# A decoder trunk with seven products for ten of eleven pairs of down projection weights, their sums made by VectorE, and another order of the token tiles

## The chip, the core and the metric

The kernel runs on one core of a Trainium2 chip. The core has TensorE (PE: matrix products, which leave their sums in eight PSUM banks of 128 x 512 floats), VectorE (DVE), ScalarE (ACT), GpSimd (POOL), and SyncE (SP), which here only issues transfers. Each engine works off its own instructions in order, and waits on the others by semaphores. The metric is the time of one execution in microseconds, lower is better.

## What is computed

A trunk of two layers over 512 tokens of 1024 floats: layer 0 mixes tokens by pooling, layer 1 by attention on keys and values that are projected from the stream after layer 0. The change lies in the feed-forward part, which each layer ends with.

```python
D_MODEL = 1024; SEQ = 512; DEPTH = 2; D_FF = 2816; CONV_WIDTH = 3

def conv_ffn(h, w_up, conv_w, conv_b, w_down):
    u = h @ w_up                              # 512x1024 @ 1024x5632
    u = causal_dwconv(u, conv_w, conv_b)      # depthwise over tokens, width 3
    a, g = jnp.split(u, 2, axis=-1)
    return (jax.nn.silu(g) * a) @ w_down      # 512x2816 @ 2816x1024

for i in range(DEPTH):
    if i == 0:
        x = x + multiscale_pool(rmsnorm(x, norm_g[i, 0]), pool_w[i], pool_scale[i])
    else:
        kv = rmsnorm(x, kv_norm) @ w_kv
        x = x + diff_attention(rmsnorm(x, norm_g[i, 0]), wq[0], lam[0], subln_g[0], wo[0], k, v, ...)
    x = x + conv_ffn(rmsnorm(x, norm_g[i, 1]), w_up[i], conv_w[i], conv_b[i], w_down[i])
return rmsnorm(x, final_norm)
```

All inputs are float32.

## The kernel before

**Products in three passes.** Every operand of a large product is split into a rounded half `hi` (ScalarE, L152) and a remainder `lo` (VectorE, L153). `mm3` then issues three matmuls: hi x hi, hi x lo, lo x hi (L171 to L173).

**Weights come in chunks** of 512 KB (`chunk`, L160): SP loads `raw` (three buffers), ScalarE makes `hi`, VectorE `lo` (rings of five buffers each). A chunk's split has to wait until TensorE has used up the chunk five places before it in the ring. Some chunks of the down projection are loaded to a "wide" tile (`wide`, L99, four buffers of 128 x 1024, tag h) in place of `raw`; the squares and scaled token tiles of the norms and the last outputs use the same four tiles.

**Up projections.** The 2816 rows of `w_down` are 22 blocks of 128, named f. For each f two chunks of `w_up` give two banks `pu` of 24 matmuls each: the gate's half and the value's half. `gate` (L387) runs the convolution on ScalarE and VectorE, then silu and the product. The first two f (`EARLY`) are made in halves of the tokens, since the second half of the tokens is normed (`sq_n`), turned by TensorE (`pt_n`) and split (`n1h`, `n1l`) while products on the first half run. `n1` is the normed input of the first FFN, `n3` that of the second, `n2` that of the attention.

**Down projection by pairs.** Two neighbouring blocks f are a pair (11 pairs, NP). A pair in plain form costs 4 token tiles x 2 halves of the output columns x 2 blocks x 3 passes. For the first `SEVEN` pairs the product is made by Strassen's scheme over two halves of the tokens (tiles 0, 1 and tiles 2, 3), two blocks of rows and two halves of columns: seven products i = 1 to 7, each on 256 tokens x 128 x 512. The left factors are "forms", sums and differences of activations: `forms_one` (L408) makes those of products 5, 6 and 3, `forms_two` (L418) those of 1, 2, 4 and 7. Forms of the first `MADE` pairs are made in the up projections (tiles `fa`, `fb`); the others are "late" and made in the down projection (tiles `hall`, and `fb`). The right factors are blocks of `w_down` or sums and differences of two blocks. Two pairs are a group g, whose weights for one product are one chunk.

**Sums of weight blocks.** `sum_weights` (L440) is called behind each gate; for products 6, 3, 7 and 4 GpSimd copies one block by a transfer to DRAM and adds the other by a second transfer (L447, `sum`), 32 transfers a layer, paced by a small POOL operation. Product 1's difference is made by VectorE in the down projection (`difference`, L484).

**Order in the down projection** (L526 to L582). First half: products 5, 6, 3 of each group, with their banks `p5`, `c2`, `p3`, then the plain pairs for column half 1. Second half: products 1, 4, 7, 2 of each group, then the plain pairs for column half 0. `put` (L510) adds a bank to the residual stream x on VectorE (L512), and `put_all` puts both banks of a product at the two places it belongs to (`PLACES`). At the end the token tiles are finished one by one, 0, 1, 2, 3: the plain pairs of a tile, its put, and `after`. In layer 0 that is `to_n2` (L586): square and norm of the tile (`vectors`), and the turning of the tile two before (`tensors`); then the value projection (`pv`, L631) begins on tiles 0 and 1, and the tiles 2 and 3 are turned between its products (L775 to L779). In layer 1 it is `finish` (L862): norm, scale and store of the output.

**What sets the order.** TensorE's order is that of the code (`manual_schedule`, L85). The start of the kernel is written by hand for all engines (`ORDER`, L30). Everything else on ScalarE, VectorE, POOL and SP is placed by the Tile scheduler, so that the diff alone doesn't tell those orders.

## Time and profile before

| what | value |
|---|---|
| time, median of 3 runs (lowest to highest) | 983.58 us (983.29 to 983.75) |
| the profiled execution: its time | 985.66 us |
| the profiled execution: its span | 983.9 us |
| granted TensorE clock, mean | 0.995 |
| TensorE matmul busy | 971.1 us, 99%, 4774 instructions |
| VectorE busy | 667.5 us, 68%, 1040 instructions |
| ScalarE busy | 464.3 us, 47%, 727 instructions |
| GpSimd busy | 152.9 us, 16%, 209 instructions |

The span is from the first to the last instruction that the profiler recorded in one execution; that execution's time holds some 1.8 us around it, and was 2.1 us above the median of the timed runs. Matmuls overlap, so a single matmul's duration is longer than the spacing of their starts, and a busy share of TensorE can be near full whatever its pace. Registers, branches and issued transfers aren't counted as busy.

### The profile page before, as it was taken

What the parts mean: (1) busy time and instruction counts of PE and PEld (TensorE: products, weight loads), DVE (VectorE), ACT (ScalarE), POOL (GpSimd) and SP (SyncE); (2) the same over time, 40 slices, a digit from 0 to 9 for tenths busy, and PEclk for the clock granted to TensorE, in tenths of its full rate; (3) what the DMA queues carried; (4) which work ended last, traced back from release to release, by engine and by line L of the source; (5) the groups of instructions that cost most, each with busy time, mean ns of one, the idle gap of its engine ahead of it and who ended that gap; (6) DMA issues with size and microseconds to landing.
All of it is one profiled execution on the core that took longest, in us unless ns stands there. A gap on an engine that the chain in (4) does not pass through costs nothing.

```text
span 983.9 us, 12623 instructions
## 1 busy us (share of the span) xinstructions
PE 971.1 (99%) x4774; PEld 822.2 (84%) x4774; DVE 667.5 (68%) x1040; ACT 464.3 (47%) x727; POOL 152.9 (16%) x209
## 2 busy tenths in 40 slices
PE   8999999999999999999999999999999999999997
PEld 8998888888888888778888887998888888888885
DVE  5777655556589756467766797686745555689764
ACT  5555433334456334346756763464433334464431
POOL 4601212121000001361220101102121212000001
PEclk8999999999999999999999999999999999999999
DMA  7335788987435532343213111336889887435422
GB/s 265 112 107 152 187 218 241 222 197 195 130 110 177 180 106 91 90 122 105 65 43 108 65 43 44 86 108 166 211 211 244 208 203 191 112 126 191 150 86 85
DMA packets 144454, 141.49 MB, mean 144 GB/s; under 512 B 4737, under 2 KB 112906, under 8 KB 144394
## 3 DMA queue, kind: packets, MB, share of 16 engines
q1 hardware_dynamic: 131082, 107.14, 34.8%
q0 software_dynamic: 13312, 33.56, 15.6%
q8 instruction: 37, 0.61, 0.2%
q14 instruction: 23, 0.19, 0.1%
HBM read 138.58 MB, written 35.65 MB: 177 GB/s over the span
## 4 chain that ended last, share of the span: by engine, by line
PE 94%; DVE 2%; DMA 1%; POOL 1%; ACT 1%; issue 1%; SPq 0%; DVEq 0%; POOLq 0%; ACTq 0%
PE pu L171 16%; PE pu L173 16%; PE pu L172 16%; PE pd L173 7%; PE pd L172 7%; PE pd L171 7%; PE sc L689 2%; PE po L718 2%; PE pw L173 2%; PE pj_k L171 1%; PE pj_k L172 1%; PE pj_k L173 1%; PE pw L172 1%; PE pw L171 1%; PE pj_q L171 1%; PE pj_q L172 1%
## 5 line engine op out<-in xcount | busy, mean ns | idle before, releaser
L153 DVE TENSOR_TENSOR lo_u<-raw_u,hi_u 128x1024 fp32r<-128x1024 f32 x84 | 103.2, 1231 | 144.2 <-ACT hi_u L152 144.0
L152 ACT CAST hi_u<-raw_u 128x1024 fp32r<-128x1024 f32 x84 | 88.3, 1053 | 147.0 <-PE pu L172 142.2
L171 PE MATMUL pu<-n3h,hi_u 128*128 128x512 f32 (+1 forms) x384 | 142.9, 372 | 0.0
L171 PE MATMUL pu<-n1h,hi_u 128*128 128x512 f32 (+1 forms) x384 | 142.8, 372 | 0.0
L172 PE MATMUL pu<-n1l,hi_u 128*128 128x512 f32 (+1 forms) x384 | 142.6, 371 | 0.0
L172 PE MATMUL pu<-n3l,hi_u 128*128 128x512 f32 (+1 forms) x384 | 142.6, 371 | 0.0
L173 PE MATMUL pu<-n1h,lo_u 128*128 128x512 f32 (+1 forms) x384 | 142.6, 371 | 0.0
L173 PE MATMUL pu<-n3h,lo_u 128*128 128x512 f32 (+1 forms) x384 | 142.6, 371 | 0.0
L173 PEld LDWEIGHTS pu<-n1h,lo_u 128*128 128x128 f32 x384 | 72.3, 188 | 12.6
L172 PEld LDWEIGHTS pu<-n3l,hi_u 128*128 128x128 f32 x384 | 72.4, 188 | 12.6
L172 PEld LDWEIGHTS pu<-n1l,hi_u 128*128 128x128 f32 x384 | 72.4, 188 | 12.5
L171 PEld LDWEIGHTS pu<-n3h,hi_u 128*128 128x128 f32 x384 | 72.3, 188 | 12.5
L173 PEld LDWEIGHTS pu<-n3h,lo_u 128*128 128x128 f32 x384 | 72.3, 188 | 12.4
L171 PEld LDWEIGHTS pu<-n1h,hi_u 128*128 128x128 f32 x384 | 72.3, 188 | 12.3
L447 POOL DMA_DIRECT2D sum<-in_w_down_dram x64 | 58.5, 913 | 150.6 <-DMA sum<-in_w_down_dram 141.9
L153 DVE TENSOR_TENSOR lo_d<-raw_d,hi_d 128x1024 fp32r<-128x1024 f32 x44 | 53.6, 1222 | 27.3 <-ACT hi_d L152 27.2
L152 ACT CAST hi_d<-raw_d 128x1024 fp32r<-128x1024 f32 x44 | 46.4, 1054 | 52.0 <-PE pd L173 36.3
L390 ACT ACTIVATE cv<-cv 128x512 f32<-128x512 f32 x44 | 27.8, 633 | 76.6 <-DVE cv L384 76.5
L171 PE MATMUL pd<-hi_d,hall 128*128 128x512 f32 x140 | 54.5, 389 | 0.0
L172 PE MATMUL pd<-lo_d,hall 128*128 128x512 f32 x140 | 54.5, 389 | 0.0
L382 ACT ACTIVATE cv<-pu,c_cb,c_cw 128x512 f32<-128x512 f32 x68 | 52.6, 774 | 0.3
L384 DVE SCALAR_TENSOR_TENSOR cv<-pu,c_cw,cv 128x510 f32<-128x510 f32 x68 | 50.9, 748 | 2.1
(197 smaller groups left out, 2035.5 us busy)
## 6 DMA issues: line engine op xcount, KB each, us to landing
raw_u<-in_w_up_dram SPq DMA_DIRECT2D x88, 512.0 KB, 4.7
sum<-in_w_down_dram POOLq DMA_DIRECT2D x64, 512.0 KB, 6.1
raw_d<-in_w_down_dram SPq DMA_DIRECT2D x28, 512.0 KB, 3.3
rs_d<-sum SPq DMA_DIRECT2D x16, 512.0 KB, 4.5
raw_d<-sum SPq DMA_DIRECT2D x16, 512.0 KB, 3.7
rs_d<-in_w_down_dram SPq DMA_DIRECT2D x8, 512.0 KB, 3.2
raw_v<-in_w_kv_dram SPq DMA_DIRECT2D x8, 512.0 KB, 3.5
raw_q<-in_wq_dram SPq DMA_DIRECT2D x8, 512.0 KB, 3.8
```

Of the source, the lines that this page charges most:

```text
L152: nc.scalar.copy(hi, src)
L153: nc.vector.tensor_tensor(lo, src, hi, ALU.subtract)
L171: nc.tensor.matmul(ps, lh, rh, start=first, stop=False)
L172: nc.tensor.matmul(ps, lh, rl, start=False, stop=False)
L173: nc.tensor.matmul(ps, ll, rh, start=False, stop=last)
L382: nc.scalar.activation(y, ps, AF.Identity, bias=w[3], scale=w[2])
L384: nc.vector.scalar_tensor_tensor(y[:, 2:], ps[:, :S - 2], w[0], y[:, 2:], ALU.mult, ALU.add)
L390: nc.scalar.activation(y, y, AF.Silu)
L447: nc.gpsimd.dma_start(out=v3(summed[g, i], 2), in_=block(g, *blk), accum_op=op)
L689: nc.tensor.matmul(ps[:, :m], qs[h, c][:, q], k[:, :m], start=not last, stop=bool(last))
L718: nc.tensor.matmul(po[h][:, qi * P:(qi + 1) * P], aT[:, kt * P:(kt + 1) * P], vt[kt][h // 4][:, (h % 4) * VD:(h % 4 + 1) * VD], start=kt = ...
```

## The change

Ten pairs in place of eight go by seven products, and the forms of four in place of three are made in the up projections. The sums of weights, with product 1's difference, are made by VectorE in ten steps during the up projections (behind the gates of f = 2, 4, ..., 20): a step takes one pair's two blocks of rows into two wide tiles (`wr`, SP), makes their sum (`wb`, L458), two sums across the columns (`wa`, L460) and a difference (into `wr`, L461) on VectorE, and POOL stores the five sums to DRAM by three transfers. A step's loads are placed on SP behind the last chunk's (`issue_after`), and the chunk loads of the down projection behind the last one of the up projections (`anchor`). In the down projection's second half the products go group by group for the first groups, then product by product for the last three (`BEHIND`), with product 7's last two groups token tile by token tile. The token tiles are finished in the order 2, 3, 0, 1 (`LAST`), and the value projection takes them in that order.

```diff
-SEVEN, MADE = 8, 3
+SEVEN, MADE = 10, 4
-SUMS = {6: ((0, 0), (0, 1)), 3: ((0, 1), (1, 1)), 7: ((1, 0), (1, 1)), 4: ((1, 0), (0, 0))}
+SUMS = 4, 3, 6, 7, 1
+LAST, BEHIND = (2, 3, 0, 1), 3
+STEPS = 2, 4, 6, 8, 10, 12, 14, 16, 18, 20
...
+    loads, anchor = [], []
     def chunk(src, a, b, name, raw=None):
...
-        nc.sync.dma_start(out=v3(raw, a), in_=src)
+        with ExitStack() as behind:
+            if anchor:
+                behind.enter_context(tc.issue_after(anchor[-1].ins))
+            loads.append(nc.sync.dma_start(out=v3(raw, a), in_=src))
...
-        def sum_weights(f, a):
-            if f < EARLY or not owing:
+        summed = [dram.tile([2 * P, len(SUMS) * S], F32, tag=f"sum{g}", bufs=2, name=f"sum{l}_{g}")
+                  for g in range(SEVEN // 2)]
+        def sum_weights(f):
+            if f not in STEPS:
                 return
-            g, i = owing.pop(0)
-            pace = nc.gpsimd.tensor_scalar(small([P, 1], f"pace{l}_{f}"), a[:, :1], 1.0, None, ALU.add)
-            with tc.issue_after(pace.ins):
-                for blk, op in zip(SUMS[i], (ALU.bypass, ALU.add)):
-                    nc.gpsimd.dma_start(out=v3(summed[g, i], 2), in_=block(g, *blk), accum_op=op)
+            kk = STEPS.index(f)
+            name = f"{l}_{kk}"
+            rows = [wide(f"wr{name}_{j}") for j in range(2)]
+            one, two = rows
+            both, across2 = wide(f"wb{name}"), wide(f"wa{name}")
+            first, last = slice(0, S), slice(S, D)
+            with tc.issue_after(loads[-1].ins):
+                for j in range(2):
+                    nc.sync.dma_start(out=rows[j], in_=w_down[l, (2 * kk + j) * P:(2 * kk + j + 1) * P, :])
+            nc.vector.tensor_tensor(both, one, two, ALU.add)
+            for r, c in (one, first), (two, last):
+                nc.vector.tensor_tensor(across2[:, c], r[:, first], r[:, last], ALU.add)
+            nc.vector.tensor_tensor(one[:, first], one[:, first], two[:, last], ALU.subtract)
+            to = summed[kk // 2][kk % 2 * P:(kk % 2 + 1) * P, :]
+            nc.gpsimd.dma_start(out=to[:, :D], in_=both)
+            nc.gpsimd.dma_start(out=to[:, D:2 * D], in_=across2)
+            nc.gpsimd.dma_start(out=to[:, 2 * D:], in_=one[:, first])
...
+        anchor.append(loads[-1])
...
-        room = {kk: [halls.pop() for _ in range(3)] for kk in range(MADE, SEVEN)}
+        room = {}
         def late_one(kk):
             if kk >= MADE:
+                room[kk] = [halls.pop() if halls else big(f"fa{l}_{kk}_{i}") for i in range(3)]
                 forms_one(kk, room[kk])
...
-        def difference(g, one, name):
-            raw, hi, lo = chunk(block(g, 1, 1), 2, S, name, wide(f"rs_{name}"))
-            nc.vector.tensor_tensor(raw, one, raw, ALU.subtract)
-            split(raw, hi, lo)
-            return hi, lo
-        def seven(i, g, w, pss, first=True, last=True):
-            for t in range(2):
+        def seven(i, g, w, pss, first=True, last=True, ts=(0, 1)):
+            for t in ts:
...
-        w0 = pair_weights(SEVEN, 1)
-        for t in (2, 3):
-            pair(c2[t - 2], t, SEVEN, w0, True)
         for g in range(SEVEN // 2):
             late_one(2 * g)
             late_one(2 * g + 1)
             seven(5, g, plain(block(g, 1, 1), f"d{l}_{g}_5")[1], p5)
-            seven(6, g, of_sum(g, 6), c2, False, False)
+            seven(6, g, of_sum(g, 6), c2, True, False)
             seven(3, g, of_sum(g, 3, True), p3)
         put_all(5, p5)
         put_all(3, p3)
         c1 = banks("12")
-        for t in (0, 1):
-            pair(c1[t], t, SEVEN, w0, True)
-        for kk in range(SEVEN + 1, NP):
+        for kk in range(SEVEN, NP):
             w = pair_weights(kk, 1)
-            late_two(MADE + kk - SEVEN - 1)
             for t in range(NT):
-                pair((c1 + c2)[t], t, kk, w, last=kk == NP - 1)
+                pair((c1 + c2)[t], t, kk, w, t < 2 and kk == SEVEN, kk == NP - 1)
...
-        for g in range(SEVEN // 2):
+        into = {1: p1, 4: p4, 2: p2, 7: c1}
+        def further(i, g):
+            w = plain(block(g, 0, 0), f"d{l}_{g}_2")[1] if i == 2 else of_sum(g, i, i == 4)
+            seven(i, g, w, into[i], True, i != 7)
+        for kk in range(MADE, MADE + NP - SEVEN):
+            late_two(kk)
+        groups = range(SEVEN // 2)
+        for g in groups:
             for kk in (2 * g, 2 * g + 1):
-                if kk >= MADE + NP - SEVEN - 1:
+                if kk >= MADE + NP - SEVEN:
                     late_two(kk)
-            raw, w2 = plain(block(g, 0, 0), f"d{l}_{g}_2")
-            w1 = difference(g, raw, f"d{l}_{g}_1")
-            end = g == SEVEN // 2 - 1
-            if end:
-                seven(2, g, w2, p2)
-            seven(1, g, w1, p1)
-            seven(4, g, of_sum(g, 4), p4)
-            seven(7, g, of_sum(g, 7, True), c1, True, False)
-            if not end:
-                seven(2, g, w2, p2)
-        put_all(2, p2)
-        put_all(1, p1, (0,))
-        put_all(4, p4, (0,))
+            if g < len(groups) - BEHIND:
+                for i in into:
+                    further(i, g)
+        for i in into:
+            for g in groups[-BEHIND:]:
+                if i != 7 or g not in groups[-2:]:
+                    further(i, g)
+            if i != 7:
+                put_all(i, into[i])
+        for t in (2, 3):
+            after(t, 1, False)
         kept = [(kk, pair_weights(kk, 0)) for kk in range(SEVEN, NP)]
+        w7 = [(g, of_sum(g, 7)) for g in groups[-2:]]
         c2 = banks("21")
-        for t in range(NT):
+        for t in LAST:
+            if t < 2:
+                for g, w in w7:
+                    seven(7, g, w, c1, True, False, (t,))
             for kk, w in kept:
                 pair((c1 + c2)[t], t, kk, w, t > 1 and kk == SEVEN, kk == NP - 1)
             put((c1 + c2)[t], t, 0)
             after(t, 0, True)
-            if t == 0:
-                put_all(1, p1, (1,))
-                put_all(4, p4, (1,))
-                for i in (2, 3):
-                    after(i, 1, False)
...
-    for t in range(NT):
+    for i, t in enumerate(LAST):
         run(value(0, t, ws))
-        if t < 2:
-            n2.tensors(t + 2)
+        if i < 2:
+            n2.tensors(LAST[i + 2])
```

VectorE's order at the start of the first FFN, before: the splits of the turned token tiles 2 and 3 (`n1l`), then that of the next weight chunk, then the first gate's convolution (`cv`).

```order
L598 TENSOR_SCALAR c_gkv<-c_gkv 128x1
L153 TENSOR_TENSOR n1l<-pt_n_620,n1h 128x4x128
L153 TENSOR_TENSOR n1l<-pt_n_625,n1h 128x4x128
L153 TENSOR_TENSOR n1l<-pt_n_630,n1h 128x4x128
L153 TENSOR_TENSOR n1l<-pt_n_635,n1h 128x4x128
L153 TENSOR_TENSOR lo_u_2_862<-raw_u_2_860,hi_u_2_861 128x1024
L383 SCALAR_TENSOR_TENSOR cv_22_788<-pu_0_560,c_cw_544,cv_22_788 128x511
```

The same place after the change:

```order
L613 TENSOR_SCALAR c_gkv<-c_gkv 128x1
L458 TENSOR_TENSOR wb_0_892<-wr_0_0_890,wr_0_1_891 128x1024
L156 TENSOR_TENSOR n1l<-pt_n_620,n1h 128x4x128
L156 TENSOR_TENSOR n1l<-pt_n_625,n1h 128x4x128
L156 TENSOR_TENSOR n1l<-pt_n_630,n1h 128x4x128
L156 TENSOR_TENSOR n1l<-pt_n_635,n1h 128x4x128
L460 TENSOR_TENSOR wa_0_893<-wr_0_0_890 128x512
L460 TENSOR_TENSOR wa_0_893<-wr_0_1_891 128x512
L461 TENSOR_TENSOR wr_0_0_890<-wr_0_0_890,wr_0_1_891 128x512
L156 TENSOR_TENSOR lo_u_2_851<-raw_u_2_849,hi_u_2_850 128x1024
```

The first step's `wb` now stands ahead of the four splits that TensorE's products on the second half of the tokens read, and the rest of the step behind them; the two loads of `wr` stand on SP's queue ahead of further chunk loads.

SP's order at the end of the up projections of layer 0, before: the last chunks of `w_up`, then those of the down projection (`sum` is the DRAM tile of sums).

```order
L166 DMA raw_u_42_2247<-in_w_up_dram 128x8x128
L166 DMA raw_u_20_2278<-in_w_up_dram 128x8x128
L166 DMA raw_u_43_2323<-in_w_up_dram 128x8x128
L166 DMA raw_u_21_2354<-in_w_up_dram 128x8x128
L166 DMA raw_d_1_8_2407<-in_w_down_dram 128x2x512
L166 DMA raw_d_0_5_2425<-in_w_down_dram 128x2x512
L166 DMA raw_d_0_6_2443<-sum_0_6_676 128x1024
L166 DMA raw_d_1_5_2486<-in_w_down_dram 128x2x512
```

The same place after the change:

```order
L174 DMA raw_u_42_2294<-in_w_up_dram 128x8x128
L174 DMA raw_u_20_2325<-in_w_up_dram 128x8x128
L457 DMA wr_9_0_2370<-in_w_down_dram 128x1024
L457 DMA wr_9_1_2371<-in_w_down_dram 128x1024
L174 DMA raw_u_43_2383<-in_w_up_dram 128x8x128
L174 DMA raw_u_21_2414<-in_w_up_dram 128x8x128
L174 DMA rs_d_0_3_2503<-sum_0_676 128x2x512
L174 DMA rs_d_1_3_2557<-sum_1_677 128x2x512
L174 DMA rs_d_2_3_2625<-sum_2_678 128x2x512
L174 DMA raw_d_0_5_2467<-in_w_down_dram 128x2x512
L174 DMA rs_d_3_3_2693<-sum_3_679 128x2x512
L174 DMA raw_d_0_6_2485<-sum_0_676 128x2x512
```

The last step's two loads stand among the last loads of `w_up`, and behind these come four chunks of product 3 (into wide tiles), ahead of or between the first chunks of products 5 and 6.

VectorE's order from the end of the down projection of layer 0 into the value projection, before: x_81 to x_84 are the token tiles 0 to 3, `x<-x,pd` is a put, `sq_n<-x` a scaling, `n2l` the split of a turned tile, `lo_v` and `lo_q` splits of weights.

```order
L209 TENSOR_SCALAR sq_n_3149<-x_81,r_n_3152 128x512 x2
L512 TENSOR_TENSOR x_82<-x_82,pd_71_2783 128x512
L209 TENSOR_SCALAR sq_n_3180<-x_82,r_n_3183 128x512 x2
L512 TENSOR_TENSOR x_83<-x_83,pd_210_3128 128x512
L153 TENSOR_TENSOR n2l<-pt_n_3215,n2h 128x4x128
L209 TENSOR_SCALAR sq_n_3207<-x_83,r_n_3210 128x512 x2
L153 TENSOR_TENSOR n2l<-pt_n_3220,n2h 128x4x128
L158 SCALAR_TENSOR_TENSOR lo_v_2_3311<-raw_v_2_3309,c_gkv,hi_v_2_3310 128x512 x2
L512 TENSOR_TENSOR x_84<-x_84,pd_211_3129 128x512
L158 SCALAR_TENSOR_TENSOR lo_v_3_3319<-raw_v_3_3317,c_gkv,hi_v_3_3318 128x512 x2
L153 TENSOR_TENSOR lo_q_3459<-raw_q_3457,hi_q_3458 128x1024
L209 TENSOR_SCALAR sq_n_3248<-x_84,r_n_3251 128x512 x2
```

The same place after the change:

```order
L217 TENSOR_SCALAR sq_n_3244<-x_83,r_n_3247 128x512 x2
L217 TENSOR_SCALAR sq_n_3259<-x_84,r_n_3262 128x512 x2
L526 TENSOR_TENSOR x_81<-x_81,pd_70_2829 128x512
L217 TENSOR_SCALAR sq_n_3286<-x_81,r_n_3289 128x512 x2
L156 TENSOR_TENSOR n2l<-pt_n_3294,n2h 128x4x128
L156 TENSOR_TENSOR n2l<-pt_n_3299,n2h 128x4x128
L161 SCALAR_TENSOR_TENSOR lo_v_2_3390<-raw_v_2_3388,c_gkv,hi_v_2_3389 128x512
L526 TENSOR_TENSOR x_82<-x_82,pd_71_2830 128x512
L161 SCALAR_TENSOR_TENSOR lo_v_2_3390<-raw_v_2_3388,c_gkv,hi_v_2_3389 128x512
L161 SCALAR_TENSOR_TENSOR lo_v_3_3398<-raw_v_3_3396,c_gkv,hi_v_3_3397 128x512 x2
L217 TENSOR_SCALAR sq_n_3327<-x_82,r_n_3330 128x512 x2
L156 TENSOR_TENSOR n2l<-pt_n_3335,n2h 128x4x128
```

The tiles 2 and 3 (x_83, x_84) are scaled first, tile 0 (x_81) next, and `n2l` of tile 2 stands behind tile 0's scaling; `lo_q` and its chunk come later.

## Rows read from the trace of the kernel before

**Rows 1.** The page, its parts 1 and 2: busy time of each engine, with the share of the span and the instructions, and the clock granted to TensorE in 40 slices, in tenths of full speed.

```profile
PE 971.1 (99%) x4774; PEld 822.2 (84%) x4774; DVE 667.5 (68%) x1040; ACT 464.3 (47%) x727; POOL 152.9 (16%) x209
...
PEclk8999999999999999999999999999999999999999
```

**Rows 2.** The waits of TensorE over the whole span, longest first: engine, line, who ended the wait; us in total, times, longest.

```profile
PE sc L689 <- DVE kl L672: 1.6, 1, 1.6
PE dps L319 <- DVE h L209: 1.4, 1, 1.4
PE warm L139 <- DVE ones L134: 1.0, 1, 1.0
PE pw L171 <- ACT oh L157: 0.8, 1, 0.8
PE pv L173 <- DVE n2l L153: 0.7, 1, 0.7
```

**Rows 3.** TensorE's timeline in the down projection of layer 0: start us, us, engine, line, operation, out<-in. The first and the last of 56 rows that follow each other without an idle time.

```profile
324.65 0.39 PE L171 MATMUL pd<-hi_d,ah 128*128 128x512 f32 x1
...
337.12 0.39 PE L172 MATMUL pd<-lo_d,fb 128*128 128x512 f32 x1
```

**Rows 4.** Busy time by stretch: the stretch, its us, then busy us (instructions) of PE, PEld, DVE, ACT and POOL, the granted clock, the DMA share and GB/s. All in layer 0: in the up projections, the fullest stretch of a pair whose forms are made there; the pair three stretches on, whose forms are made later; the rest of the up projections; then the first half of the down projection.

```profile
63.30:85.00 21.70, 21.70 (x97) 17.98 (x96) 16.98 (x25) 10.58 (x16) 2.12 (x3) 1.00 0.48 141
128.60:150.30 21.70, 21.70 (x97) 18.00 (x96) 11.92 (x14) 8.12 (x11) 5.12 (x7) 1.00 0.79 204
150.30:280.90 130.60, 130.60 (x577) 108.12 (x577) 75.71 (x92) 52.24 (x67) 18.29 (x27) 1.00 0.72 189
280.90:318.50 37.60, 37.60 (x167) 31.16 (x166) 37.27 (x58) 23.74 (x33) 0.00 (x0) 1.00 0.46 157
```

**Rows 5.** Groups of instructions between 278 and 400 us, different shapes kept apart: line, engine, operation, out<-in, count | busy us, mean ns of one | idle time before them. The last row is from the page's part 5, of the whole span.

```profile
L153 DVE TENSOR_TENSOR lo_d<-raw_d,hi_d 128x1024 fp32r<-128x1024 f32 x19 | 23.1, 1221 | 7.8 <-ACT hi_d L152 7.8
L512 DVE TENSOR_TENSOR x<-x,pd 128x512 f32<-128x512 f32 x28 | 17.9, 681 | 0.8 <-PE pd L173 0.6
L153 DVE TENSOR_TENSOR hall<-f,hall 128x512 fp32r<-128x512 f32 x5 | 3.4, 682 | 0.0
L412 DVE TENSOR_TENSOR f<-ar 128x256 f32<-128x256 f32 x5 | 2.1, 418 | 0.0
...
L384 DVE SCALAR_TENSOR_TENSOR cv<-pu,c_cw,cv 128x510 f32<-128x510 f32 x68 | 50.9, 748 | 2.1
```

**Rows 6.** The page's parts 5 and 6 on the splits of the up weights and on the loads, with the median us from issue to landing; and what the trace has of line 447, POOL's transfers (ns: shortest, median, longest).

```profile
L153 DVE TENSOR_TENSOR lo_u<-raw_u,hi_u 128x1024 fp32r<-128x1024 f32 x84 | 103.2, 1231 | 144.2 <-ACT hi_u L152 144.0
L152 ACT CAST hi_u<-raw_u 128x1024 fp32r<-128x1024 f32 x84 | 88.3, 1053 | 147.0 <-PE pu L172 142.2
...
raw_u<-in_w_up_dram SPq DMA_DIRECT2D x88, 512.0 KB, 4.7
sum<-in_w_down_dram POOLq DMA_DIRECT2D x64, 512.0 KB, 6.1
...
L447 POOL DMA_DIRECT2D sum<-in_w_down_dram x64: 738/966/1091, 78.6 to 834.6; - x64
```

**Rows 7.** Timeline of ScalarE and VectorE late in the up projections of layer 0: one chunk's split on both engines, and the next one's on VectorE.

```profile
247.79 1.05 ACT L152 CAST hi_u<-raw_u 128x1024 fp32r<-128x1024 f32 x1 [0.96 <-PE pu L172]
...
248.88 1.23 DVE L153 TENSOR_TENSOR lo_u<-raw_u,hi_u 128x1024 fp32r<-128x1024 f32 x1 [2.77 <-ACT hi_u L152]
254.31 1.22 DVE L153 TENSOR_TENSOR lo_u<-raw_u,hi_u 128x1024 fp32r<-128x1024 f32 x1 [0.66 <-ACT hi_u L152]
```

**Rows 8.** Timeline at the start of the first FFN: SP's issues, VectorE's split of the transposed token tiles 2 and 3, and on TensorE their transposes and the first product that reads them (the products between go on with tiles 0 and 1).

```profile
41.90 0.39 SPq L166 DMA_DIRECT2D raw_u<-in_w_up_dram  x1
...
47.94 2.48 DVE L153 TENSOR_TENSOR n1l<-pt_n,n1h 128x512 fp32r<-128x512 f32 x4 [2.31 <-ACT n1h L152]
...
46.69 1.91 PE L236 MATMUL pt_n<-ident,sq_n 128*128 128x128 f32 x16
...
51.31 0.28 PE L171 MATMUL pu<-n1h,hi_u 128*128 128x256 f32 x1
```

**Rows 9.** Timeline from the end of the down projection of layer 0 into the value projection: SP's load of raw_q; POOL; VectorE's scaling of token tiles 1 and 3 and the n2l behind the latter; TensorE's wait.

```profile
376.92 0.37 SPq L166 DMA_DIRECT2D raw_q<-in_wq_dram  x1
...
382.35 1.90 POOL L641 TENSOR_TENSOR raw_q<-raw_q,c_gn 128x1024 f32<-128x1024 f32 x1 [2.25 <-DMA raw_q<-in_wq_dram]
384.64 0.57 POOL L194 TENSOR_TENSOR r_n<-r_n,halfneg 128x1 f32<-128x1 f32 x1
395.64 2.13 POOL L641 TENSOR_TENSOR raw_k<-raw_k,c_gkv 128x1024 f32<-128x1024 f32 x1
...
385.24 0.88 DVE L209 TENSOR_SCALAR sq_n<-x,r_n 128x512 f32<-128x512 f32 x2 [3.26 <-POOL r_n L194]
395.52 2.52 DVE L209 TENSOR_SCALAR sq_n<-x,r_n 128x512 f32<-128x512 f32 x2 [0.77 <-POOL r_n L194]
397.97 2.47 DVE L153 TENSOR_TENSOR n2l<-pt_n,n2h 128x512 fp32r<-128x512 f32 x4
...
398.70 0.50 PE L173 MATMUL pv<-hi_v,n2l 128*128 128x512 f32 x1 [0.69 <-DVE n2l L153]
```

**Rows 10.** Timeline of the last microseconds: the last matmul, and the last step on VectorE of the chain behind it.

```profile
976.27 0.39 PE L173 MATMUL pd<-hi_d,al 128*128 128x512 f32 x1
...
979.22 1.42 DVE L875 SCALAR_TENSOR_TENSOR y<-x,fr,fg 128x512 f32<-128x512 f32 x2 [1.83 <-POOL fr L871]
```

More of the change, by code (lines that the diff above doesn't have):

```diff
@@ L401, in gate @@
                 act[f] = ah, al
-            sum_weights(f, a)
+            sum_weights(f)
         left, right = slice(0, HALF), slice(HALF, S)
@@ L432, in block @@
             return src.rearrange("(k j p) c -> j p k c", j=2, p=P)[j]
-        summed = {(g, i): dram.tile([P, 2 * S], F32, tag=f"sum{g}_{i}", bufs=2, name=f"sum{l}_{g}_{i}")
-                  for i in SUMS for g in range(SEVEN // 2)}
-        owing = list(summed)
-        def sum_weights(f, a):
-            if f < EARLY or not owing:
-                return
-            g, i = owing.pop(0)
-            pace = nc.gpsimd.tensor_scalar(small([P, 1], f"pace{l}_{f}"), a[:, :1], 1.0, None, ALU.add)
-            with tc.issue_after(pace.ins):
-                for blk, op in zip(SUMS[i], (ALU.bypass, ALU.add)):
-                    nc.gpsimd.dma_start(out=v3(summed[g, i], 2), in_=block(g, *blk), accum_op=op)
+        summed = [dram.tile([2 * P, len(SUMS) * S], F32, tag=f"sum{g}", bufs=2, name=f"sum{l}_{g}")
+                  for g in range(SEVEN // 2)]
+        def sum_weights(f):
+            if f not in STEPS:
+                return
+            kk = STEPS.index(f)
[15 more added lines that the diff above has]
+            nc.gpsimd.dma_start(out=to[:, 2 * D:], in_=one[:, first])
         for n, w in enumerate(ws):
@@ L481, in of_sum @@
         def of_sum(g, i, other=False):
-            return plain(v3(summed[g, i], 2), f"d{l}_{g}_{i}", other)[1]
-        def difference(g, one, name):
-            raw, hi, lo = chunk(block(g, 1, 1), 2, S, name, wide(f"rs_{name}"))
-            nc.vector.tensor_tensor(raw, one, raw, ALU.subtract)
-            split(raw, hi, lo)
-            return hi, lo
-        def seven(i, g, w, pss, first=True, last=True):
-            for t in range(2):
+            at = SUMS.index(i) * S
+            return plain(summed[g].rearrange("(k p) c -> p k c", p=P)[:, :, at:at + S], f"d{l}_{g}_{i}", other)[1]
+        def seven(i, g, w, pss, first=True, last=True, ts=(0, 1)):
+            for t in ts:
                 for k in range(2):
@@ L577, in ffn @@
             after(t, 0, True)
-            if t == 0:
-                put_all(1, p1, (1,))
-                put_all(4, p4, (1,))
-                for i in (2, 3):
-                    after(i, 1, False)
+        anchor.clear()
     n2 = Normed("n2", None)
@@ L589, in to_n2 @@
         n2.vectors(t)
-        if t > 1:
-            n2.tensors(t - 2)
+        if t in LAST[2:]:
+            n2.tensors(LAST[LAST.index(t) - 2])
     ffn(0, n1, cw0, [w[1:] for w in up0], pup, to_n2)
```

## The prediction, made before the changed kernel ran

> **What bounds the kernel now.** I read the busy shares first, then what TensorE waited for, then single rows. TensorE's matmul row is busy 99% of the span, at a granted clock of full speed in all slices but the first [rows 1]. A busy share alone proves little, as matmuls overlap, so the second look is at the waits: the five of the whole span add to 5.5 us, and the two that lie behind the first FFN are 1.6 and 0.7 us [rows 2]; none lies inside an up or a down projection. The third look is at the spacing of starts. In the down projection 56 matmuls of 512 columns stand in a row without a gap, from 324.65 to 337.12 us: 12.47 / 55 = 0.2267 us each [rows 3]. So a matmul taken out there is worth 0.2267 us as long as its neighbours' operands are ready, and what has to be asked of this change is whether they stay ready.
>
> **Matmuls removed.** A pair of weight rows costs 48 matmuls of 512 columns in plain form (4 token tiles, 2 dim halves, 2 row blocks, 3 passes) and 42 in seven products (7 products, 2 tiles, 2 blocks, 3 passes). Two more pairs go over to seven products, in two layers: 2 x 2 x 6 = 24 matmuls, and TensorE's program is 24 rows shorter. 24 x 0.2267 = **5.44 us**. This is sure; the rest of the working is what may be lost of it.
>
> **VectorE in the up projections.** A step (one pair's sums) is one 128x1024 and three 128x512 two-input operations. By the nearest rows, lo_d at 1221 ns and x at 681 ns [rows 5], that is 1.22 + 3 x 0.68 = 3.3 us, ten times a layer, where an inner step lies 21.8 us from the next. VectorE was busy at most 17.0 us of 21.7 while a pair's forms are made, 11.9 of 21.7 in the fourth pair, and 75.7 of 130.6 afterwards [rows 4]. The fourth pair now makes its forms there too: 0.42 x 3 + 0.68 for one half and 0.42 + 3 x 0.68 for the other [rows 5], 4.4 us. So the fullest stretches are 17.0 + 3.3 = 20.3 and 11.9 + 4.4 + 3.3 = 19.6 of 21.7 us: below full, though not by much. A delay there is covered besides: the split of a weight chunk waits for ScalarE, ScalarE waits for TensorE [rows 6], and the rows show the rhythm: hi_u begins 0.96 us after its wait began, when a chunk has been used up, 1.05 and 1.23 us later the chunk is ready [rows 7], and the ring has five places, so it is used four chunks of 24 x 0.2267 = 5.44 us later. That is some 21.8 - 2.3 = 19.5 us of lead. I take 0 for these operations; uncovered they would cost 65 us (20 x 3.3).
>
> **The queues.** A step also issues two 512 KB loads on SP and three stores on POOL. Before, POOL issued 32 copying or adding transfers a layer at 966 ns each [rows 6]; now 30 plain ones. The four wide tiles that a step uses are all there are, so the next step's loads, in SP's queue ahead of raw_u loads, wait until the stores have landed. The chain of one step, from the rows: loads 4.7 us, VectorE 3.3 plus what stands ahead of it there (up to some 5), three issues 2.9, landing 6.1 [rows 5, 6]: about 22 us at the worst, 17 at best, against 21.8 between steps. At the worst it just keeps step, and being late first eats the lead. 0 again.
>
> **Start of the first FFN.** Here the cover is thin. VectorE's new order has wb_0 ahead of the four n1l. The loads that wb_0 needs are issued where a raw_u was, at 41.9 and some 0.5 us later, and its tile comes free with the first eight of 16 transposes, at about 46.69 + 0.95 = 47.6 [rows 8]. With the landing of the same size, 4.7 us [rows 6], the data are there at 47.1; so wb_0 runs 47.6 to 48.8, the third n1l (spacing 2.48 / 4 = 0.6) is done at 50.7, and TensorE wants it from 51.43, one matmul after 51.31 [rows 8]. Nothing is lost. Bounds: no loss, and, with a landing of 9.4 us (twice the row), data at 51.8 and a loss of 51.8 + 1.2 + 1.9 - 51.4 = 3.5 us. I take 0, the nearest row.
>
> **Down projection.** First half now: 15 products of 12 matmuls, 40.8 us, with 15 splits (18.3 us), six late forms of 1.94 us (11.6), and the end of the last gates (4 operations of 0.75, two of 0.68 [rows 5]): 34.3 us of VectorE. Before, VectorE was busy 37.3 of 37.6 us there and TensorE had no gap [rows 4]. The plain pair that held one place of the ring through this half is gone, so the lead grows by one product, 2.7 us. Between the halves only one plain pair (5.4 us) is left where 60 matmuls (13.6 us) stood; the first product after it needs the banks of product 5, which ended two products earlier, and its four puts take 2.7 us; the next needs those of product 3, which has 5.4 + 2.7 us for as many puts. Second half: the eight 1.22 us differences of both layers go, the late forms are started in the first half by the new order, and chunk loads stay one per product. I take 0; the bound is one late product's puts, 2.7 us a layer.
>
> **Token order 2, 3, 0, 1 at the end of layer 0.** Before, TensorE lost 0.69 us in the value projection: n2l of token tile 1 stood in VectorE's queue behind the scaling of tile 3, which waited for POOL, and whose second half took over 2 us beside POOL's raw_k [rows 9]. In the new order tiles 2 and 3 cost TensorE 1.4 us each, and the two long ones (4.1 us) follow, so that the scaling of 2 and 3 is hidden under tile 0. The raw_q load can issue some 9 us before tile 1 ends; with its 5.4 us (376.92 to 382.35) and POOL's 1.9 and 0.9 us [rows 9] tile 0's scaling ends close to where TensorE reaches the value projection, and n2l of tile 2 is behind it, ready at about the moment it is read. raw_k's load is issued later than before, after lo_v_2, and should not meet the scaling of tile 1. So the old 0.69 goes, and 0 to 1.7 comes (1.7: the collision again, 2.1 - 0.5). I take a gain of 0.3.
>
> **Tail.** After the last matmul the chain put, square, rstd, scale, store is the same [rows 10], for tile 1 in place of 3: 0.
>
> **Sum.** 5.44 + 0.3 = 5.7 us of the profiled execution's 985.66 us (span 983.9): 979.9. The median of the timed runs is 983.58, lower by 2.1, and it is that which is forecast: 983.58 - 5.7 = **977.9 us**.
>
> [...] In [rows 9] a scaling of 128x512 that otherwise takes under 0.5 us took over 2 us while POOL read SBUF: the two engines do hold each other up. [...]
>
> **Rivals.**
> *Part is given back* at the thin places: start and value projection. For it: both leads are below 1 us. 983.58 - 5.44 + 1 to 3.5 = 979.1 to 981.6.
> *Nothing measurable is left:* puts of the first half late in both layers, 2 x 2.7 = 5.4 us, so 983.6. Against it: banks of product 5 come free early.
> *Slower, the wide tiles.* If a step's chain takes longer than the 21.8 us between steps, SP stands still before raw_u loads and each step adds to the delay. Nine steps eat the 19.5 us lead when the chain is over 21.8 + 19.5 / 9 = 24 us. At 25.5 us: 9 x 3.7 - 19.5 = 13.8 us a layer, 983.58 - 5.44 + 27.6 = 1005.7 us. For it: the sums' landing of 6.1 us and the hold-up in [rows 9]. Against it: behind the fourth pair VectorE keeps some 27% of idle time with the step in it (75.7 + 6 x 3.3 of 130.6 us [rows 4]), and POOL has nothing else to do there.
>
> **Chances.** Forecast (976.6 to 979.1) 0.66; part given back 0.18; nothing left 0.08; slower 0.08. For eight times in ten the first two are enough: 976.6 (all of 5.44, 0.69 and 0.8 for what may shrink elsewhere) to 981.6. Within 0.2% (2 us) is about what a measurement of this kernel can't tell from no change; 981.6 is its edge, so the first two count as faster, 0.84, then 0.08 same and 0.08 slower.
>
> **What would show it.** The waits should hold no wait of pd or pu over 1 us; the spacing in the down projection should still be 0.227 us, with 12 matmuls fewer a layer; VectorE busier by 30 to 40 us a layer; the pv wait gone or small; POOL's transfers still near 0.9 us. Wrong would be: a wait of pu on lo_u or on a raw_u load in the up projections (wide tiles), a wait of pu on n1l near 51 us (start), a wait of pd on a put or a split after the first half.

## The result, and the profile after

The changed kernel takes 979.0 us (median of 5 runs, 977.73 to 979.26), the kernel before 983.75 us (983.29 to 984.38): a ratio of 0.995, 95% interval 0.9935 to 0.9964, so 4.75 us less. Two further measurements on other chips gave ratios of 0.9942 and 0.9946 (experiments `a_again`, `a_third`).

The page of the changed kernel, parts 1 and 2, as in [rows 1]:

```profile
PE 965.3 (99%) x4750; PEld 817.0 (84%) x4750; DVE 725.8 (74%) x1142; ACT 473.9 (48%) x741; POOL 120.4 (12%) x173
...
PEclk9999999999999999999999999999999999999999
```

The waits of TensorE over the whole span, as in [rows 2]:

```profile
PE pp L180 <- DVE pwl L156: 1.1, 2, 0.9
PE warm L142 <- DVE ones L137: 1.0, 1, 1.0
PE dps L327 <- DVE h L217: 0.8, 1, 0.8
PE pw L179 <- ACT oh L160: 0.8, 1, 0.8
PE pp L179 <- ACT pwh L155: 0.5, 1, 0.5
PE pu L180 <- DVE n1l L156: 0.3, 1, 0.3
```

TensorE's matmul is busy 5.8 us less, VectorE 58.3 us more, POOL 32.5 us less. The waits of pv and sc of [rows 2] are gone. Behind the first up product one wait is new, and it is one that the prediction priced at nothing: pu for n1l, 0.3 us. Those on pp, dps and warm lie ahead of the first up product, where every engine's order is the same in both kernels; the one on pw is there in both.

The spacing in the down projection, two rows of TensorE's timeline in layer 0, the first and the last of 56 without idle time between, as in [rows 3]:

```profile
323.43 0.39 PE L180 MATMUL pd<-lo_d,ah 128*128 128x512 f32 x1
...
335.90 0.39 PE L181 MATMUL pd<-hi_d,fb 128*128 128x512 f32 x1
```

12.47 us / 55 = 0.2267 us, as before. To see where the 4.75 us came from, the starts of each stage's first and last matmul are read from TensorE's timeline in several profiles: of the kernel before (a second profile of it is `b_again`), of the changed one (two more are `a_again` and `a_third`), and of the version with later steps (`e3_later`). The rows run from a stage's first matmul to its last, by their starts (those of the value projection and of the scores to the first of the next stage); what lies between the rows is the same in all. All in us:

| stretch | before | b_again | after | a_again | a_third | e3_later |
|---|---|---|---|---|---|---|
| to the first up product | 37.33 | 37.58 | 38.03 | 36.85 | 36.85 | 37.01 |
| up projections, layer 0 | 242.90 | 242.89 | 243.47 | 244.50 | 245.23 | 242.89 |
| down projection, layer 0 | 109.48 | 109.48 | 106.76 | 106.76 | 106.76 | 106.76 |
| value projection | 24.65 | 24.69 | 23.69 | 23.69 | 23.69 | 23.69 |
| first scores to layer 1's FFN | 184.66 | 183.08 | 183.06 | 183.05 | 183.06 | 183.06 |
| up projections, layer 1 | 242.73 | 242.73 | 242.73 | 242.73 | 242.73 | 242.73 |
| down projection, layer 1 | 108.57 | 108.57 | 105.85 | 105.85 | 105.85 | 105.85 |
| last matmul to the span's end | 7.63 | 7.62 | 7.76 | 7.72 | 7.78 | 7.76 |

Four rows differ by kernel. The two down projections are shorter by 2.72 us each, to the hundredth in every profile. The value projection is 0.96 us shorter. The up projections of layer 0 are longer by 0.57, 1.61 and 2.34 us, 1.5 on the mean. The tail is 0.1 us longer. That makes -5.44 - 0.96 + 1.5 + 0.1 = -4.8 us, the measured difference. Of these six profiles only the first one of before has the 1.6 us among the scores, and the start differs by a microsecond between profiles of one kernel (38.03 and 36.85), so it is left out of the sum.

### The profile page after: what moved, and what is told of

Its sections match the earlier page's. It is cut to its first block, busy times and chain, and to the rows that moved or that the text cites. A ratio compares the mean times of both kernels' runs of the same rounds, so it can differ in the third digit from the quotient of the medians.

```text
span 977.3 us, 12805 instructions
## 1 busy us (share of the span) xinstructions
PE 965.3 (99%) x4750; PEld 817.0 (84%) x4750; DVE 725.8 (74%) x1142; ACT 473.9 (48%) x741; POOL 120.4 (12%) x173
## 5 line engine op out<-in xcount | busy, mean ns | idle before, releaser
L156 DVE TENSOR_TENSOR lo_d<-raw_d,hi_d 128x1024 fp32r<-128x1024 f32 x54 | 65.9, 1224 | 35.0 <-ACT hi_d L155 35.0
L155 ACT CAST hi_d<-raw_d 128x1024 fp32r<-128x1024 f32 x54 | 57.1, 1057 | 63.2 <-PE pd L181 43.3
L179 PE MATMUL pd<-hi_d,hall 128*128 128x512 f32 x156 | 60.8, 390 | 0.0
L180 PE MATMUL pd<-lo_d,hall 128*128 128x512 f32 x156 | 60.7, 389 | 0.0
L458 DVE TENSOR_TENSOR wb<-wr,wr 128x1024 f32<-128x1024 f32 x20 | 24.5, 1224 | 36.8 <-DMA wr<-in_w_down_dram 36.8
L390 ACT ACTIVATE cv<-pu,c_cb,c_cw 128x512 f32<-128x512 f32 x64 | 49.5, 773 | 0.5 <-PE pu L181 0.5
L392 DVE SCALAR_TENSOR_TENSOR cv<-pu,c_cw,cv 128x510 f32<-128x510 f32 x64 | 47.9, 748 | 1.5
```

The source lines that it names most:

```text
L155: nc.scalar.copy(hi, src)
L156: nc.vector.tensor_tensor(lo, src, hi, ALU.subtract)
L179: nc.tensor.matmul(ps, lh, rh, start=first, stop=False)
L180: nc.tensor.matmul(ps, lh, rl, start=False, stop=False)
L390: nc.scalar.activation(y, ps, AF.Identity, bias=w[3], scale=w[2])
L392: nc.vector.scalar_tensor_tensor(y[:, 2:], ps[:, :S - 2], w[0], y[:, 2:], ALU.mult, ALU.add)
```

## Where the new wait comes from

SP's timeline of the changed kernel at the start of the first FFN (start us, us, operation, count), then VectorE's, ScalarE's `n1h`, then TensorE's first product that reads the third n1l; they answer to [rows 8]:

```profile
42.62 0.83 SPq L457 DMA_DIRECT2D wr<-in_w_down_dram  x2
43.55 0.38 SPq L174 DMA_DIRECT2D raw_u<-in_w_up_dram  x1
...
49.52 1.23 DVE L458 TENSOR_TENSOR wb<-wr,wr 128x1024 f32<-128x1024 f32 x1 [3.19 <-DMA wr<-in_w_down_dram]
50.67 2.48 DVE L156 TENSOR_TENSOR n1l<-pt_n,n1h 128x512 fp32r<-128x512 f32 x4
...
48.02 2.06 ACT L155 CAST n1h<-pt_n 128x512 fp32r<-128x512 f32 x4 [5.31 <-PE pt_n L244]
...
52.60 0.39 PE L180 MATMUL pu<-n1l,hi_u 128*128 128x256 f32 x1 [0.32 <-DVE n1l L156]
```

And busy time by stretch at this place: PE, PEld, DVE, ACT, POOL, granted clock, DMA share, GB/s:

```profile
42.00:46.00 4.00, 4.00 (x36) 4.00 (x35) 3.29 (x10) 0.71 (x2) 2.57 (x4) 1.00 0.86 266
46.00:48.00 2.00, 2.00 (x19) 2.00 (x19) 0.33 (x2) 0.00 (x0) 0.00 (x0) 1.00 0.96 335
48.00:50.00 2.00, 2.00 (x20) 2.00 (x19) 0.47 (x1) 1.98 (x4) 0.00 (x0) 1.00 0.74 227
```

The two loads of `wr` are issued at 42.62 us and right behind, and `wb` begins at 49.52, 6.9 us behind the first one's issue, where 5.7 us were forecast (41.9 to 47.6). Three loads of 512 KB now stand where one stood, and the transfer engines are 96% and 74% busy in the stretches 46 to 48 and 48 to 50 us; in the kernel before they were at 7% and nothing. That the loads are slow because they stand together is read from these shares; no run took one of the three away. VectorE stands still for 3.19 us ahead of `wb`, with the four n1l behind it, whose operands come ready from ScalarE's `n1h`, begun at 48.02. In `a_third` the same rows read:

```profile
42.41 0.83 SPq L457 DMA_DIRECT2D wr<-in_w_down_dram  x2
...
50.11 1.23 DVE L458 TENSOR_TENSOR wb<-wr,wr 128x1024 f32<-128x1024 f32 x1 [4.80 <-DMA wr<-in_w_down_dram]
...
53.19 0.39 PE L180 MATMUL pu<-n1l,hi_u 128*128 128x256 f32 x1 [2.08 <-DVE n1l L156]
```

There `wb` begins 7.7 us after the first load's issue, and TensorE, which was earlier by 1.2 us at its first up product, waits 2.1 us. So an early start isn't kept: it ends in this wait.

## The experiments

**The matmuls: eight pairs as before, with three pairs' forms made early and eight steps of sums; everything else changed.**

```diff
-SEVEN, MADE = 10, 4
+SEVEN, MADE = 8, 3
-STEPS = 2, 4, 6, 8, 10, 12, 14, 16, 18, 20
+STEPS = 2, 4, 6, 8, 10, 12, 14, 16
```

> The changed kernel with eight pairs by seven products and three with forms made early, as before; everything else of the change stays (VectorE's sums in eight steps, the new product order, the new token order). Theory A (the gain is the 24 matmuls at 0.2267 us, the rest of the change nearly cancels: 1.0 us gained at the value projection, 0.6 us lost at the start): 5.4 us above the changed kernel's 979.0, so 984.4 us, each down projection 2.72 us longer than the changed kernel's 106.8 and 105.9 us. Theory B (the gain comes from the other edits, the order of products and tiles): within 1 us of 979.0.

Measured: 987.1 us (986.79 to 988.98). The two down projections take 109.48 and 108.57 us, 2 x 2.72 above the changed kernel, as theory A has it. It is off by 2.7 us elsewhere, of which 1.9 us lie in the value projection, where this mixture of old and new has a wait of its own. Two of TensorE's waits:

```profile
PE pv L180 <- DVE lo_v L161: 1.3, 1, 1.3
...
PE pu L180 <- DVE n1l L156: 0.9, 1, 0.9
```

and VectorE and POOL ahead of that wait:

```profile
395.76 3.05 DVE L161 SCALAR_TENSOR_TENSOR lo_v<-raw_v,c_gkv,hi_v 128x512 fp32r<-128x512 f32 x2
...
395.95 2.30 POOL L656 TENSOR_TENSOR raw_q<-raw_q,c_gn 128x1024 f32<-128x1024 f32 x1 [1.03 <-DVE sq_n L217]
```

The two `lo_v` (0.75 us for one when nothing stands beside it) took 3.05 us while POOL scaled `raw_q`. So without the 24 matmuls the rest of the change is a loss in this mixture: 987.1 us against 983.72 of the kernel before on that chip.

**Token order alone, in the changed kernel.**

```diff
-LAST, BEHIND = (2, 3, 0, 1), 3
+LAST, BEHIND = (0, 1, 2, 3), 3
```

> The changed kernel with the token tiles finished in the old order 0, 1, 2, 3. Theory A (the order 2, 3, 0, 1 hides the norms of the first two tiles under the two long tiles): TensorE waits in the value projection for an n2l or n2h, 0.7 to 2.5 us, and the time is 979.7 to 981.5 us. Theory B (the order is worth nothing, the wait of 0.7 us in the kernel before was an accident of VectorE and POOL meeting): 978.7 to 979.3 us and no wait of pv over 0.3 us.

Measured: 986.69 us (985.48 to 988.73), far above both theories' figures. TensorE waits for the scaling of the last two tiles before it can turn them:

```profile
PE pt_n L244 <- DVE sq_n L217: 3.8, 2, 2.3
```

The end of layer 0's down projection and the way to the value projection are 1.74 + 2.51 us longer than in the changed kernel. Another 2.9 us lie behind the last matmul, which theory A had not thought of: VectorE's rows there are

```profile
975.56 1.41 DVE L890 SCALAR_TENSOR_TENSOR y<-x,fr,fg 128x512 f32<-128x512 f32 x2 [0.45 <-POOL fr L886]
976.89 0.68 DVE L526 TENSOR_TENSOR x<-x,pd 128x512 f32<-128x512 f32 x1
```

The last put (976.89) could start at 973.85, when the last matmul ends, but stands behind the output of the tile before, which waits for POOL. In the order 2, 3, 0, 1 the last tile comes 4.1 us after the one before it and its put begins 0.1 us after the last matmul.

**Token order alone, in the kernel before.**

```diff
-        put_all(1, p1, (0,))
-        put_all(4, p4, (0,))
+        put_all(1, p1)
+        put_all(4, p4)
+        for t in (2, 3):
+            after(t, 1, False)
...
-        for t in range(NT):
+        for t in (2, 3, 0, 1):
```

> The kernel before with one part of the change alone: its token tiles end in the order 2, 3, 0, 1 (puts of products 1 and 4 all ahead of the first tile, the value projection in the same order); here each of the four tiles still costs TensorE 4.1 us. Theory A (the new order is worth something by itself): the wait of 0.7 us in the value projection is gone, which with the slow restart behind it is 0.96 us, so 982.8 us against 983.7. Theory B (the old order was good for the old, even tiles; the new one only suits the new, uneven ones): no change within 0.5 us, 983.3 to 984.2 us, a wait there or at the tail as often as before.

Measured: 985.61 us (984.13 to 987.72), ratio 1.0013 (1.0003 to 1.0022): 1.1 us slower, so neither theory. In its profile the stages are those of before but for an earlier start (36.35 us) and the value projection, 25.75 us in place of 24.65. That execution was the fastest of the twelve; what the slower ones hold, up to 987.72 us, is not shown. The wait of 0.7 us became one of 1.8:

```profile
PE pv L174 <- DVE n2l L154: 1.8, 1, 1.8
```

and its cause is that of [rows 9], the last tile's scaling beside POOL's `raw_k`:

```profile
395.63 2.52 DVE L210 TENSOR_SCALAR sq_n<-x,r_n 128x512 f32<-128x512 f32 x2 [0.77 <-POOL r_n L195]
398.08 2.47 DVE L154 TENSOR_TENSOR n2l<-pt_n,n2h 128x512 fp32r<-128x512 f32 x4
...
395.78 2.09 POOL L639 TENSOR_TENSOR raw_k<-raw_k,c_gkv 128x1024 f32<-128x1024 f32 x1 [0.18 <-DMA raw_k<-in_w_kv_dram]
```

So the order as such is worth nothing here; in the kernel before each tile costs TensorE the same 4.1 us. What matters is whether that scaling meets POOL's work. In the changed kernel it doesn't:

```profile
393.53 0.89 DVE L217 TENSOR_SCALAR sq_n<-x,r_n 128x512 f32<-128x512 f32 x2 [0.77 <-POOL r_n L202]
...
395.60 2.90 POOL L656 TENSOR_TENSOR raw_k<-raw_k,c_gkv 128x1024 f32<-128x1024 f32 x1 [2.10 <-DMA raw_k<-in_w_kv_dram]
```

Its two halves take 0.89 us together, POOL's `raw_k` begins 2.1 us later. Which of the edits keeps the two apart isn't isolated by a run.

**Steps one f later.**

```diff
-STEPS = 2, 4, 6, 8, 10, 12, 14, 16, 18, 20
+STEPS = 3, 5, 7, 9, 11, 13, 15, 17, 19, 21
```

> The changed kernel with every step of sums one f later (f = 3, 5, ..., 21), so that no wb stands ahead of the four n1l at the start of the first FFN. Theory A (wb waiting for its loads held up the third n1l by 0.57 us): the wait of pu for n1l is gone, the up projections of layer 0 take 242.9 us in place of 243.5, the time is 978.4 us. Theory B (0.57 us lies within what the start varies by, and the later last step makes product 3's chunks late): 979.0 us or more, with a wait of pd in the first half.

> The changed kernel with its steps of sums one f later, on one chip with the changed kernel itself. Theory A (wb, waiting for its loads ahead of the four n1l, costs 0.6 to 1.6 us, more when the kernel's start is early): no wait of pu for n1l, up projections of layer 0 in 242.9 us, and a median 1.0 to 1.6 us below the changed kernel's. Theory B (what is saved there is lost again later): medians within 0.5 us.

Measured: 977.9 us (976.79 to 981.14), and in the second measurement 977.86 us (976.96 to 979.56) beside the changed kernel's 980.0 us on the same chip. That is 2.1 us less, more than the 1.0 to 1.6 expected, and the two ranges overlap (the changed kernel's is 977.62 to 981.37), so the size rests on the stages rather than on the medians. The ratios to the kernel before are 0.9945 (0.9933 to 0.9957) and 0.993 (0.9914 to 0.9946). The wait for n1l is gone in both profiles and layer 0's up projections take 242.89 us. The loads of the first step stand at nearly the same time, 42.13 us, behind one load of `raw_u` more; what moved is `wb`, behind the n1l:

```profile
42.13 1.37 SPq L457 DMA_DIRECT2D wr<-in_w_down_dram  x2
...
47.62 2.48 DVE L156 TENSOR_TENSOR n1l<-pt_n,n1h 128x512 fp32r<-128x512 f32 x4 [2.31 <-ACT n1h L155]
50.02 1.22 DVE L458 TENSOR_TENSOR wb<-wr,wr 128x1024 f32<-128x1024 f32 x1
```

It doesn't wait for its data there, and TensorE doesn't wait for it. Of all kernels run this has the lowest medians.

**Twice the work on VectorE, twice the stores.** In the first, `wb` and both `wa` of a step are made twice; in the second, the three stores of a step are issued twice.

```diff
+            for _ in range(2):
-            nc.vector.tensor_tensor(both, one, two, ALU.add)
+                nc.vector.tensor_tensor(both, one, two, ALU.add)
...
```

```diff
+            for _ in range(2):
-            nc.gpsimd.dma_start(out=to[:, :D], in_=both)
+                nc.gpsimd.dma_start(out=to[:, :D], in_=both)
...
```

> The changed kernel with wb and both wa of each step made twice (52 us more VectorE work, 2.6 us a step; the result is the same). The fullest stretches then want 22.9 and 22.2 us of VectorE in 21.7. Theory A (the lead of 12 to 20 us of a weight chunk's split covers it): 979.0 us, at the start up to 0.6 us more. Theory B (VectorE at its limit in the first pairs delays the splits until TensorE waits): 4 stretches of 1.2 us over and the delays of both layers show, waits of pu for lo_u, 982 to 990 us.

> The changed kernel with each of a step's three stores issued twice (60 more transfers of 256 to 512 KB; the result is the same), so the four wide tiles come free later. Theory A (12 to 20 us of lead of the up weights' splits cover it): 979.0 us within 0.7, the first step's stores on POOL may shift nothing. Theory B (the chain of one step just keeps pace with 21.8 us between steps, so SP stands before the next step's loads and the up weights come late): waits of pu for lo_u or raw_u, 982 us or more.

Measured: 980.55 us (979.69 to 981.54) and 978.94 us (978.35 to 980.15). Layer 1's up projections take 242.73 us in both, as everywhere. Those of layer 0 are longer by 1.96 and 1.63 us, which is the wait for n1l (1.7 and 1.4 us, and the slower matmuls around it: in `e4_double` the starts on its two sides lie 1.98 us apart and the next two 0.22, where 0.12 is usual), the size that it has without the extra work too. The first one's profile also holds the wait for `kl` at the first scores that [rows 2] has; whether its timed runs have it is open, and with it the 1.5 us between its median and the changed kernel's, which theory A didn't have. VectorE is busy 770.3 us there, 44.5 more than in the changed kernel, where 52 were expected. The two stretches that were to want 22.9 and 22.2 us have 20.51 and 18.23; the fullest lies between them:

```profile
85.00:106.80 21.80, 21.80 (x98) 18.06 (x97) 21.46 (x31) 9.93 (x14) 1.76 (x4) 1.00 0.67 222
```

In the up projections themselves this work cost nothing where there is lead, and neither did 60 more transfers.

**The same two kernels again.**

> The kernel before, unchanged, for a second profile. Theory A (the wait of 1.6 us for kl at the first scores came from a chance meeting of VectorE and POOL, not from the kernel's order): it is gone or of another size in this profile, and the span is about 982.0 us; the wait of 0.7 us in the value projection is there again. Theory B (both belong to the kernel's order): both waits are there, span 983.9 us.

> The changed kernel, unchanged, for a second profile. Theory A (the first up product began 0.7 us later than before by chance): it begins at 37.0 to 37.6 us here as in four of the five other profiles, and the median is 978.3 us. Theory B (the change itself moves the start, by other loads on SP or longer programs): 38.0 us again, median 979.0 us. The wait for n1l of 0.3 us is there in both.

> The changed kernel, unchanged, beside the one with later steps. Theory A: the wait of pu for n1l is there, 0.3 to 1.4 us, and wb begins some 6.5 to 7.5 us after its second load was issued; median 978.5 to 979.5 us. Theory B: no such wait in this profile, median as with later steps.

Measured: 984.64 us (983.56 to 987.03) for before, 978.93 (977.47 to 980.11) and 980.0 us (977.62 to 981.37) for the change. In `b_again` the wait for `kl` is missing, that of the value projection is there, and the span is 982.6 us. VectorE and POOL at the first scores, in the profile shown ahead of the prediction:

```profile
438.48 2.82 DVE L153 TENSOR_TENSOR lo_q<-raw_q,hi_q 128x1024 fp32r<-128x1024 f32 x1 [1.86 <-ACT hi_q L152]
...
438.31 1.90 POOL L641 TENSOR_TENSOR raw_q<-raw_q,c_gn 128x1024 f32<-128x1024 f32 x1 [1.42 <-DMA raw_q<-in_wq_dram]
```

and in `b_again`:

```profile
438.76 1.23 DVE L153 TENSOR_TENSOR lo_q<-raw_q,hi_q 128x1024 fp32r<-128x1024 f32 x1 [1.46 <-ACT hi_q L152]
...
439.52 2.22 POOL L641 TENSOR_TENSOR raw_q<-raw_q,c_gn 128x1024 f32<-128x1024 f32 x1 [1.94 <-DMA raw_q<-in_wq_dram]
```

The same split of `raw_q` takes 2.82 us when POOL has begun its next scaling 0.17 us earlier, and 1.23 us when VectorE is first by 0.76 us. Which comes first differs between these two profiles of one kernel; the wait of 1.6 us was theory A's accident. In `e4_double` POOL began 0.04 us ahead, and the split took 2.94 us, with the same wait behind it. For `a_again` the start was even earlier than theory A's 37.0 to 37.6 (36.85 us), and its median was wrong: the start that was won went into the wait for n1l, 1.3 us. In `a_third` that wait is 2.1 us, and the median 980.0, both more than theory A gave it.

## Why the prediction was right, and where it wasn't

**Matmuls: right.** 5.44 us forecast, 2 x 2.72 measured, in three profiles of either side.

**VectorE in the up projections: right.** The fullest stretches were forecast at 20.3 and 19.6 us of 21.7; measured in the same two, by stretch as in [rows 4], the last row being the first half of the down projection:

```profile
63.30:85.00 21.70, 21.70 (x102) 18.09 (x101) 20.52 (x29) 10.76 (x16) 1.61 (x3) 1.00 0.68 229
128.60:150.30 21.70, 21.70 (x98) 17.96 (x97) 16.35 (x25) 9.84 (x14) 1.62 (x3) 1.00 0.53 172
150.30:280.90 130.60, 130.60 (x578) 108.15 (x577) 88.85 (x109) 50.04 (x62) 8.09 (x15) 1.00 0.64 209
281.70:322.60 40.90, 40.90 (x182) 33.85 (x181) 39.74 (x62) 26.77 (x37) 0.00 (x0) 1.00 0.57 171
```

20.52 and 16.35 us, the second 3.2 us below its forecast. Over the whole span VectorE is busier by 29 us a layer, just under the 30 to 40 forecast. No split of an up weight was late, and in `e4_double` none is with VectorE busy 21.46 of 21.8 us.

**The queues: right on the cost, mis-sized on the length of a step.** POOL's stores take 0.53 to 0.56 us of issue (the first of each layer more, 0.79 at most), not 0.97, and their median landings are 2.9 to 4.1 us. The rows of the page's part 6:

```profile
raw_u<-in_w_up_dram SPq DMA_DIRECT2D x88, 512.0 KB, 4.4
wr<-in_w_down_dram SPq DMA_DIRECT2D x40, 512.0 KB, 6.0
...
sum<-wb POOLq DMA_DIRECT2D x20, 512.0 KB, 2.9
sum<-wa POOLq DMA_DIRECT2D x20, 512.0 KB, 3.5
...
sum<-wr POOLq DMA_DIRECT2D x20, 256.0 KB, 4.1
```

One step of layer 0, from its loads' issue at 103.18 us to its last store's landing at about 121.5 (117.41 and the median of 4.1), takes 18 us where 17 to 22 were forecast. But the steps differ: reckoned so, the twenty take 14 to 25 us, and five of them more than the 22 that were to be the worst. The longest, in layer 1:

```profile
683.82 0.97 SPq L457 DMA_DIRECT2D wr<-in_w_down_dram  x2
...
704.32 0.55 POOL L465 DMA_DIRECT2D sum<-wr  x1
```

With 4.1 us that is 24.6 us, past the 24 us at which the rival *slower, the wide tiles* has nine steps eat the lead. One alone did, and the steps late in each layer take 14. SP's waits at L457 are 0.9 us in all, for the transposes and not for a store, so by the profile no step's loads stood before a tile that was still being stored:

```profile
SPq L457 <- PE pt_n L244: 0.9, 1, 0.9
```

The hold-up in [rows 9], which that rival counts for itself, doesn't show for POOL's transfers: they keep their 0.53 to 0.56 us of issue with VectorE 68 to 95% busy in the stretches of the up projections above. About two thirds of VectorE's time in those stretches is `tensor_tensor`; no run here has another kind of operation in its place. What the case does show is the hold-up between VectorE and POOL's arithmetic: two `lo_v` in 3.05 us where one takes 0.75 (`e1_seven8`), a scaling in 2.52 us where it takes 0.88 (`b_2301`, and so in the first profile of before, [rows 9]), a split in 2.82 us where it takes 1.23 (the same profile), and on POOL's side a scaling in 2.22 us where it takes 1.90 (`b_again`).

**The start: the step that failed.** The prediction put the landing of `wr` at 4.7 us, the median of the up weights' loads, and so `wb` at 47.6 us and the loss at 0. It gave 3.5 us as the bound with twice that landing. The loads were issued about as forecast, but the second took 6.4 to 7.5 us from its issue until `wb` could begin, beside the third load in the same stretch, and `wb` began at 49.4 to 50.1 us in the three profiles. The loss was 0.6 to 2.3 us, 1.5 on the mean, and the wait of pu on n1l that the prediction named as a sign of being wrong is there in all three. The rival *part is given back* named this place, and here it is what happened, though at the other place that it named more was won. That the sum stays inside the forecast's own range (976.6 to 979.1) is luck: the gain at the value projection, three times what was forecast, made up for part of this loss.

**Down projection: right on the time, off on the cover.** No wait, 0.2267 us. But VectorE was busy 39.74 of 40.9 us in the first half, not 34.3: the 15 splits are there as forecast, but besides the six late forms five puts and some forms for products of the second half stand there too, which the working left out. It was as full as before, and still not late.

**Token order: right in sign, mis-sized.** 0.3 us taken, 0.96 us measured (the wait of 0.7 us and the slower matmuls around it: in the first profile of before the starts on its two sides lie 1.08 us apart and the next two 0.34, where 0.23 is usual). The argument that the two long tiles hide the scaling of the short ones holds for the changed kernel (1.74 + 2.51 us lost there without it, `e2_order0123`), and the old wait's cause, POOL beside the last scaling, was read rightly; `b_2301` shows that the order without uneven tiles doesn't remove it. (The bound of a loss, 2.1 - 0.5, is 1.6 and not 1.7.)

**The tail: 0 forecast, 0.1 us longer.**

**The base of the sum: right.** The difference went from the median and not from the profiled execution, which lay 2.1 us above it; 1.6 us of that were the accident at the first scores.

## What to carry to other kernels

When an operation that waits for a load is placed ahead of others in an in-order queue, price the load by the traffic that the change itself adds at that place, not by the median of single loads over the program; and if work has slack, put it behind what has none (here one step in f was worth 1.5 us, by the stages). An order of tiles is worth what its tiles are: judge it by how long the last ones take and by what stands on the other engines at that time. And before a wait in one profile is counted as something to win, look whether a second profile has it.

## What the runs showed of the hardware that was not expected

A 512 KB load took 4.4 us from issue to landing as a median of the up weights. Of three issued within 1.3 us the second's data were used 6.4 to 7.5 us after its issue, with the transfer engines 96% busy for 2 us of it in the changed kernel's profile; the 40 loads of `wr`, which come in twos, have a median landing of 6.0. And VectorE's subtraction on 128x1024 took 1.23 us by itself and 2.82 us beside POOL's multiplication on 128x1024, which had begun 0.17 us before it; when VectorE's began 0.76 us ahead, it kept its 1.23 us and POOL's took 2.22 in place of 1.90. The 2.82 us end 1.09 us after POOL's operation does (441.30 and 440.21). Five more splits on 128x1024 in the first profile of before began 0.72 to 1.16 us after a scaling of POOL's did; they took 1.82 to 2.80 us and ended 1.08 to 1.09 us after it. That is 0.14 to 0.15 us less than the 1.23 us of a split by itself; what holds the split up until then, no run shows.
